# A two-layer decoder trunk in float32 on one core: a new order of work at three layer handovers and at the start

## Chip, core and metric

The kernel runs on one core of a Trainium2 chip (trn2). The metric is device time in microseconds of one execution of the whole program; lower is better. TensorE (PE) multiplies matrices, VectorE (DVE) and ScalarE (ACT) do the elementwise work, SyncE (SP) issues nearly all DMA transfers, GpSimd (POOL) a few.

## What is computed

A batch of one sequence, 256 tokens of width 2048, goes through two layers. Each layer is a mixer followed by a SwiGLU feed-forward of inner width 5632; every sublayer has an RMS norm in front (with shift and scale that depend on a vector `c`) and another one behind it (with a gate that depends on `c`).

```python
for layer in range(DEPTH):                       # DEPTH = 2
    sh1, sc1, g1, sh2, sc2, g2 = split(silu(c) @ mod_w[layer] + mod_b[layer])
    h = rms_norm(x, norm_g[layer, 0]) * (1 + sc1) + sh1
    y = nsa_mixer(h, ...) if layer == 0 else sb_mixer(h, k_sh, v_sh, ...)
    x = x + g1 * rms_norm(y, norm_g[layer, 1])
    h = rms_norm(x, norm_g[layer, 2]) * (1 + sc2) + sh2
    y = (silu(h @ W_gate) * (h @ W_up)) @ ffn_w_out[layer]
    x = x + g2 * rms_norm(y, norm_g[layer, 3])
```

Layer 0 mixes with block-sparse attention (compressed, selected and windowed keys), layer 1 with stick-breaking attention on keys and values that are projected once from the stream that leaves layer 0. All weights are float32 in HBM, 657 MB are moved in all.

## The kernel before

**Products.** Tokens are two tiles t = 0 and t = 1 of 128. A weight block is 512 rows by 512 columns (1 MB). It is loaded as `raw`; ACT copies it into `wh`, rounded to a shorter format, and DVE writes `wl` = raw - wh. Activations are split into a high and a low part in the same way. One unit is one weight block times one token tile: four 128-row pieces with three matmuls each (high·wh, high·wl, low·wh), 12 matmuls of 128x512 that add into one PSUM bank `acc`. The activation operands are called `hA`, `oA`, `hhF`, `hhK`, `hhB`, `oB`, `fa`; each has four chunks kt = 0 to 3 of 512 columns.

**Order of the work.** At build time a planner (class `Emit`, lines 149 to 422) lays down every instruction. It keeps a clock per engine from cost formulas, starts the next unit on PE when its plan has weights, operand and bank, and runs epilogues as coroutines (`run_bg`). `pump` (line 333) decides when the next weight block is split (`wq`), when a modulation row block is processed (`mq`), and when the next load is issued; pages of SBUF (21 of 8 KB per partition) are shared by loads, splits, activations and the rest. Where the plan has PE idle for over 1.2 us and a bank free, `fill` (line 194) puts in small matmuls on a scratch bank, named `idle`. On the chip only the order and the semaphores count.

**A handover** (`residual`, line 922) is the stretch between one sublayer's last product and the next one's first, and there are three: attention output to feed-forward in layer 0 (operand `hhF`), feed-forward of layer 0 to the key/value projection (`hhK`), attention output to feed-forward in layer 1 (`hhF`). For each token tile the chain is: sum of squares of the last block (`junk`), gate product (`z` or `yp`), reduce, square root, four updates of the residual stream `X` with their sums of squares, reduce, square root, reciprocal, four scaled chunks `xn`, 16 transposes on PE into `xT`, then per chunk four scale-and-shift operations `hf`, a rounding copy and a subtraction (`h_tile`, line 809; `split`, line 762). Tile 0 of a sublayer's last column block is multiplied four units ahead of tile 1 (`emit_lag`, line 1414), so tile 0's chain runs under tile 1's last 48 matmuls, and tile 1's chain under tile 0's first 48 of the next sublayer. While `E.urgent` is set, from the end of tile 0's product until tile 1's chunks are done, `pump` splits blocks in halves and stops when three units ahead have their weights:

```python
if self.wq and not (self.urgent and self.ahead > URGENT):      # URGENT = 2
```

When tile 0's first accumulator of the next sublayer ends, its epilogue is started at once (`after`, line 1671); for a feed-forward that is a silu on ACT (`sg`), for the key/value projection a copy (`pt`) and four transposes.

**Loads** are held back so that splits find pages:

```python
hold = 2 * max(0, self.reserve - len(self.ready)) + self.wait_pages
```

**Start** (lines 471 to 510). SP issues eight small loads, then `x` in two halves of 1 MB, three loads of constants, one of a bias, and then the modulation blocks `modq` (1 MB each) whose products with silu(c) give the first shift and scale; the first product of the kernel waits for four of them.

Of the kernel before, what the change touches and what calls it, by code (L numbers as in the profile page):

```python
# [18 lines left out]
P = 128  # L19
# [37 lines left out]
URGENT = 2  # L57
# [92 lines left out]
class Emit:  # L150
# [4 lines left out]
    def __init__(self, nc):  # L155
        self.now = 0.0
        self.clk = dict(PE=0.0, ACT=0.0, DVE=0.0, DMA=0.0, DMA2=0.0)
# [20 lines left out]
        self.urgent = False  # L178
# [5 lines left out]
        self.D = Engine(self, "DMA", nc.sync)  # L184
        self.D2 = Engine(self, "DMA2", nc.gpsimd)
# [147 lines left out]
    def pump(self):  # L333
# [4 lines left out]
        if self.wq and not (self.urgent and self.ahead > URGENT):  # L338
# [110 lines left out]
def kernel(ctx: ExitStack, tc, consts, x, c, mod_w, mod_b, norm_g, ffn_w_in, ffn_w_out, a_w_in,  # L449
# [43 lines left out]
    DMA.dma_start(L0[:, 0:512], consts[:, C_COS:C_END])  # L493
    DMA.dma_start(w2, a_cmp_w2[0].rearrange("s (m p) d -> p s m d", p=P))
    DMA.dma_start(gb[0:3 * H], a_gate_b.rearrange("o r -> r o"))
# [6 lines left out]
    for r in range(2):  # L502
        V.tensor_copy(maskb[:, r], cm[:, C_MASK - C_KEEP:C_MASK - C_KEEP + P])
    V.tensor_copy(maskTb, cm[:, C_MASKT - C_KEEP:C_MASKT - C_KEEP + P])
    for t in range(2):
        for r in range(4):
            V.tensor_copy(cmpb[:, t, r], cm[:, C_CMP - C_KEEP + 16 * t:C_CMP - C_KEEP + 16 * t + 16])
    E.put("s2")
    E.filler = (identb, maskb.rearrange("p r n -> p (r n)"))
# [287 lines left out]
    def xT_block(t, kt, r):  # L797

        xn = yield from E.get("s2", "xn")
        scaled(xn, X[:, t, kt * NB:(kt + 1) * NB], r)  # L800
# [8 lines left out]
    def h_tile(name, t, kt, r, a, sh):  # L809

        b = yield from xT_block(t, kt, r)
        dst = (yield from page_of((name, kt), "h" + name))[:, :, :, t * P:(t + 1) * P]
        hf = yield from E.get("s2", "hf")
        for j in range(4):
            cc = kt * 4 + j
            affine(hf[:, j * P:(j + 1) * P], b[:, j * P:(j + 1) * P], a[:, cc:cc + 1], sh[:, cc:cc + 1])
        E.put("x")
        split(dst, hf.rearrange("p (j n) -> p j n", j=4))
        E.put("s2")
        E.flag((name, kt, t))  # L820

    def h_all(name, t, r, a, sh, deps, pause=None):
        yield from E.wait(*deps)
        for kt in range(KT):
# [3 lines left out]
            else:  # L828
                E.spawn(h_tile(name, t, kt, r(), a, sh))
# [92 lines left out]
    def residual(key, t, nxt, final=False):  # L922
# [25 lines left out]
        if not final:  # L948
# [4 lines left out]
            if t == 1:  # L953
                yield from E.wait(*[(name, kt, 1) for kt in range(KT)])
                E.urgent = False
# [662 lines left out]
    E.spawn(start_norm())  # L1618
    E.spawn(make_xpe(0))
# [25 lines left out]
    def mm_unit(i, u):  # L1645
# [8 lines left out]
        def piece(j):  # L1654
# [9 lines left out]
            if j == js[-1]:  # L1664
                if u["stop"]:
                    E.spawn(after(u["epi"](accs.pop(u["acc"]), t, u["nb"]), E.fin + 0.1), front=True)
# [4 lines left out]
    def after(gen, t):  # L1671
        yield t
        yield from gen
# [73 lines left out]
```

## Time and profile before

| | |
|---|---|
| median of 3 runs | 2462.58 us (2462.18 to 2463.68) |
| profiled execution, its own time | 2461.23 us |
| its span, first to last instruction | 2459.4 us |
| PE busy | 97% of the span |
| DVE busy | 67% |
| ACT busy | 43% |
| DMA queue of SP | 73.4% of 16 engines, 651.59 MB |
| the chain that ended last | PE 84%, DVE 7%, ACT 4%, DMA 2% |

The time of an execution is its span and 1.8 us around it. A matmul's recorded duration overlaps that of the next one, so PE counts as busy through gaps that are shorter than a record; where PE really stood still is read from start times in the timeline. Small filler matmuls count as busy too.

### The profile page before, as it was taken

To read this page: it belongs to the slowest core of one execution; us is meant where nothing else is said; L and a number is where in the kernel's file an instruction comes from. 1 tells how busy PE (TensorE), PEld (TensorE's weight loads), DVE (VectorE), ACT (ScalarE), POOL (GpSimd) and SP (SyncE) were. 2 spreads that over 40 slices of the span, in tenths; PEclk is the share of its full clock that TensorE was granted. 3 is DMA by queue.
4 is the path that set the end of the run, shared out by engine and by line. 5 is a ranking of instruction groups with operands and counts; after the bars stand their busy time and mean duration, and the time that the engine had idled before them with its cause. 6 is when DMAs were issued, how large, how long until landed. Compare 5 with 4: busy or idle time off the path is not lost.

```text
span 2459.4 us, 27413 instructions
## 1 busy us (share of the span) xinstructions
PE 2387.1 (97%) x11238; PEld 1927.8 (78%) x11238; DVE 1638.2 (67%) x1373; ACT 1067.2 (43%) x1191; POOL 4.9 (0%) x12
## 2 busy tenths in 40 slices
PE   5999999999999999999999999999999999999998
PEld 3667776778888888888877888888788888888887
DVE  3788788968677667767768687666644544554554
ACT  3433444464333344333445365655433333433342
POOL 0000000000000000000000000000000000000000
PEclk9999999999999999999999999999999999999999
DMA  9996966868987689977667979675665646865642
GB/s 338 389 386 215 354 240 241 302 244 329 349 296 276 238 292 398 342 283 285 246 232 280 392 248 382 234 266 188 232 220 199 205 154 223 309 205 198 211 171 103
DMA packets 265629, 657.56 MB, mean 267 GB/s; under 512 B 12448, under 2 KB 30112, under 8 KB 240160
## 3 DMA queue, kind: packets, MB, share of 16 engines
q1 hardware_dynamic: 264800, 651.59, 73.4%
q0 software_dynamic: 704, 4.23, 0.5%
q8 instruction: 88, 1.44, 0.2%
q14 instruction: 37, 0.30, 0.0%
HBM read 653.64 MB, written 2.13 MB: 267 GB/s over the span
## 4 chain that ended last, share of the span: by engine, by line
PE 84%; DVE 7%; ACT 4%; DMA 2%; SPq 1%; issue 1%; DVEq 0%; ACTq 0%
PE acc L118 77%; DVE wl L118 2%; DVE macc L118 2%; PE z L118 1%; SPq L118 1%; ACT wh L118 1%; DMA modw<-in_mod_w_dram 1%; PE aT L118 1%; ACT hf L118 1%; PE oT L118 1%; PE sc L118 1%; ACT junk L118 1%; PE qacc L118 1%; PE pmod L118 1%; PE xT L118 1%
## 5 line engine op out<-in xcount | busy, mean ns | idle before, releaser
L118 DVE TENSOR_TENSOR wl<-raw,wh 128x2048 fp32r<-128x2048 f32 (+2 forms) x392 | 878.8, 2249 | 539.2 <-ACT wh L118 499.3
L118 ACT ACTIVATE wh<-raw 128x2048 fp32r<-128x2048 f32 (+2 forms) x392 | 732.8, 1880 | 653.1 <-PE acc L118 426.5
L118 PE MATMUL acc<-wh,hhF 128*128 128x512 f32 x2816 | 881.2, 391 | 0.0
L118 PEld LDWEIGHTS acc<-wh,hhF 128*128 128x128 f32 x2816 | 528.5, 188 | 113.7 <-issue 4.2
L118 PE MATMUL acc<-wl,hhF 128*128 128x512 f32 x1408 | 548.0, 389 | 0.0
L118 DVE SCALAR_TENSOR_TENSOR macc<-modw,cact,macc 128x2048 f32<-128x2048 f32 x180 | 422.4, 2347 | 44.5 <-DMA modw<-in_mod_w_dram 34.2
L118 PE MATMUL acc<-wh,fa 128*128 128x512 f32 x1408 | 437.1, 390 | 0.0
L118 PEld LDWEIGHTS acc<-wh,fa 128*128 128x128 f32 x1408 | 264.3, 188 | 55.5 <-issue 0.8
L118 PEld LDWEIGHTS acc<-wl,hhF 128*128 128x128 f32 x1408 | 264.5, 188 | 53.5
L118 PE MATMUL acc<-wl,fa 128*128 128x512 f32 x704 | 273.9, 389 | 0.0
L118 PE MATMUL acc<-wh,hA 128*128 128x512 f32 x640 | 222.6, 408 | 2.8 <-DVE hA L118 1.7
L118 PE MATMUL acc<-wh,hhK 128*128 128x512 f32 x512 | 164.1, 396 | 2.4 <-ACT hhK L118 1.8
L118 PEld LDWEIGHTS acc<-wh,hA 128*128 128x128 f32 x640 | 122.1, 191 | 44.6 <-issue 18.7
L118 PEld LDWEIGHTS acc<-wl,fa 128*128 128x128 f32 x704 | 132.2, 188 | 27.2
L118 PE MATMUL acc<-wl,hA 128*128 128x512 f32 x320 | 127.3, 398 | 2.0 <-DVE wl L118 2.0
L118 PEld LDWEIGHTS acc<-wh,hhK 128*128 128x128 f32 x512 | 96.8, 189 | 24.1 <-ACT hhK L118 2.0
L118 PE MATMUL acc<-wl,hhK 128*128 128x512 f32 x256 | 100.6, 393 | 2.3 <-DVE wl L118 2.3
L118 ACT ACTIVATE fa<-aT 128x512 fp32r<-128x512 f32 x44 | 26.0, 593 | 170.6 <-PE aT L118 158.6
L118 PE MATMUL acc<-wh,oA 128*128 128x512 f32 x256 | 84.9, 402 | 0.0
L118 PE MATMUL acc<-wh,hhB 128*128 128x512 f32 x256 | 84.8, 398 | 0.0
L118 PE MATMUL acc<-wh,oB 128*128 128x512 f32 x256 | 81.8, 394 | 0.0
L118 PEld LDWEIGHTS acc<-wl,hA 128*128 128x128 f32 x320 | 61.4, 192 | 13.5 <-DVE wl L118 3.6
(182 smaller groups left out, 1700.5 us busy)
## 6 DMA issues: line engine op xcount, KB each, us to landing
raw<-in_ffn_w_in_dram SPq DMA_DIRECT2D x176, 1024.0 KB, 5.4
modw<-in_mod_w_dram SPq DMA_DIRECT2D x160, 1024.0 KB, 7.2
raw<-in_ffn_w_out_dram SPq DMA_DIRECT2D x88, 1024.0 KB, 5.2
raw<-in_a_w_in_dram SPq DMA_DIRECT2D x40, 1024.0 KB, 13.0
modq<-in_mod_w_dram SPq DMA_DIRECT2D x32, 1024.0 KB, 14.1
modw<-in_kv_mod_w_dram SPq DMA_DIRECT2D x32, 1024.0 KB, 5.9
raw<-in_kv_w_dram SPq DMA_DIRECT2D x32, 1024.0 KB, 9.1
raw<-in_a_w_out_dram SPq DMA_DIRECT2D x16, 1024.0 KB, 7.4
```

The source lines that it names most:

```text
L118: return f(*a, **k)
```

## The change

Five edits, in one diff.

1. A sublayer's first operand chunk (kt = 0) is made first and in two steps of 256 columns, and its first half is enough to start PE. Its scaled copy `xn` is always DVE's.
2. `E.urgent` gets two levels. Level 1 (tile 0's chain) no longer stops weight splits; level 2 (tile 1's chain) does as before.
3. The epilogue of tile 0's first accumulator in the two feed-forwards and the key/value projection waits until the handover is over.
4. `hold` counts only as many missing splits as there are loads on their way or waiting for a split.
5. At the start `x` is issued from ACT's DMA queue, and the constants, `w2` and the bias behind the first seven blocks instead of ahead of them.

```diff
-URGENT = 2
+URGENT = (9, 9, 2)
...
-        if self.wq and not (self.urgent and self.ahead > URGENT):
+        if self.wq and self.ahead <= URGENT[self.urgent]:
...
-            hold = 2 * max(0, self.reserve - len(self.ready)) + self.wait_pages
+            hold = 2 * max(0, min(self.reserve - len(self.ready), len(self.wq) + 0)) + self.wait_pages
...
+    E.DA.dma_start(X[:, 0], xv[:, 0])
+    E.DA.dma_start(X[:, 1], xv[:, 1])
...
-    DMA.dma_start(X[:, 0], xv[:, 0])
-    DMA.dma_start(X[:, 1], xv[:, 1])
-    DMA.dma_start(cm[:, 0:C_COS - C_KEEP], consts[:, C_KEEP:C_COS])
...
+    def late_consts():
+
+        while E.dma_ptr < 6:
+            yield False
+        DMA.dma_start(cm[:, 0:C_COS - C_KEEP], consts[:, C_KEEP:C_COS])
+        DMA.dma_start(L0[:, 0:512], consts[:, C_COS:C_END])
+        DMA.dma_start(w2, a_cmp_w2[0].rearrange("s (m p) d -> p s m d", p=P))
+        DMA.dma_start(gb[0:3 * H], a_gate_b.rearrange("o r -> r o"))
+        yield E.when(cm)
...
-        scaled(xn, X[:, t, kt * NB:(kt + 1) * NB], r)
+        if first:
+            V.tensor_scalar(xn, X[:, t, kt * NB:(kt + 1) * NB], r, None, op0=OP.mult)
+        else:
+            scaled(xn, X[:, t, kt * NB:(kt + 1) * NB], r)
...
+        for i in range(0, 4, 2 if first else 4):
+            js = range(i, i + (2 if first else 4))
+            for j in js:
+                cc = kt * 4 + j
+                affine(hf[:, j * P:(j + 1) * P], b[:, j * P:(j + 1) * P], a[:, cc:cc + 1], sh[:, cc:cc + 1])
+            split(dst[:, :, js.start:js.stop], hf.rearrange("p (j n) -> p j n", j=4)[:, js.start:js.stop])
+            if i == 0:
+                E.flag((name, kt, t))
...
-            E.urgent = True
+            E.urgent = 1
...
+            E.urgent = 2
...
+                    first = u["acc"][0] in ("g0", "g1", "kv") and u["nb"] == 0 and t == 0
+                    E.spawn(after(u["epi"](accs.pop(u["acc"]), t, u["nb"]), E.fin + 0.1, first), front=True)
...
-    def after(gen, t):
+    def after(gen, t, calm=False):
         yield t
+        while calm and E.urgent:
+            yield False
```

**First place: the start.** SP's order before, from the constants that PE's first transposes need (`K`); the numbers behind a name tell buffers of one kind apart:

```order
L118 DMA K<-in_consts_dram 128x260
L118 DMA X<-in_x_dram 128x2048 x2
L118 DMA cmask_69<-in_consts_dram 128x288
L118 DMA L_3_82<-in_consts_dram 128x512
L118 DMA L_3_82<-in_a_cmp_w_dram 128x4x128
L118 DMA gb<-in_a_gate_b_dram 48x1
L118 DMA modq_134<-in_mod_w_dram 128x8x256
```

The same stretch of SP's order now:

```order
L118 DMA K<-in_consts_dram 128x260
L118 DMA modq_119<-in_mod_w_dram 128x8x256
L118 DMA modq_121<-in_mod_w_dram 128x8x256
L118 DMA modq_123<-in_mod_w_dram 128x8x256
L118 DMA raw_125<-in_a_w_in_dram 128x4x512
L118 DMA modq_127<-in_mod_w_dram 128x8x256
L118 DMA raw_129<-in_a_w_in_dram 128x4x512
L118 DMA modq_131<-in_mod_w_dram 128x8x256
L118 DMA cmask_69<-in_consts_dram 128x288
L118 DMA L_3_81<-in_consts_dram 128x512
L118 DMA L_3_81<-in_a_cmp_w_dram 128x4x128
L118 DMA gb<-in_a_gate_b_dram 48x1
```

And ACT's first instructions now, with the semaphore that each waits for (DMAHW0 is the one that the first half of `x` raises when it has landed):

```order
L118 DMA X<-in_x_dram 128x2048
L118 DMA X<-in_x_dram 128x2048 [waits DMAHW0_49]
L118 ACT_TABLE_LOAD
L118 ACTIVATE cact<-vecT 128x16 [waits DVE_49]
```

Both halves of `x` went to ACT's queue, the second behind the landing of the first, and three constant loads and the bias went behind seven blocks.

**Second place: the first handover on DVE.** Before, from tile 0's last operand chunk to the reduce that begins tile 1's chain (`z_3636` is tile 1's last gate product; `wl` of 128x1024 is half a split):

```order
L118 TENSOR_TENSOR hhF_682_4006<-hf_4007,hhF_682_4006 128x4x128
L118 TENSOR_TENSOR wl_4027<-raw_3873,wh_4026 128x1024
L118 TENSOR_TENSOR z_3636<-acc_3890,G_3105 128x512
L118 TENSOR_TENSOR wl_4027<-raw_3873,wh_4026 128x1024
L118 TENSOR_TENSOR wl_4049<-raw_3932,wh_4048 128x1024 x2
L118 TENSOR_REDUCE stat<-stat 128x1
```

Now, tile 0's first chunk (the first row is its last scaled copy):

```order
L118 TENSOR_SCALAR xn_3978<-X,stat 128x512
L118 TENSOR_TENSOR wl_3981<-raw_3896,wh_3980 128x1024
L118 TENSOR_TENSOR hhF_678_3987<-hf_3988,hhF_678_3987 128x2x128
L118 CAST hhF_678_3987<-hf_3988 128x2x128
L118 TENSOR_TENSOR hhF_678_3987<-hf_3988,hhF_678_3987 128x2x128
```

and from its last chunk to the reduce:

```order
L118 TENSOR_TENSOR hhF_685_4021<-hf_4022,hhF_685_4021 128x4x128
L118 TENSOR_TENSOR wl_3981<-raw_3896,wh_3980 128x1024
L118 TENSOR_TENSOR z_3617<-acc_3898,G_3150 128x512
L118 TENSOR_TENSOR wl_4062<-raw_3933,wh_4061 128x1024 x2
L118 TENSOR_REDUCE stat<-stat 128x1
```

One half split moved from between `z` and the reduce to the place ahead of tile 0's first chunk; two are left behind `z` where three were.

**Third place: the first handover on ACT, tile 1.** Before, from the scaled copy on (`sg` is the silu of the feed-forward's first accumulator):

```order
L118 ACTIVATE xn_4106<-X,stat 128x512
L118 ACT_TABLE_LOAD
L118 ACTIVATE sg_4120<-acc_4030 128x512
L118 ACTIVATE hf_4155<-xT_4133,mall 128x128 x3
L118 ACTIVATE hf_4162<-xT_4138,mall 128x128 x3
```

Now:

```order
L118 ACTIVATE xn_4116<-X,stat 128x512
L118 ACTIVATE hf_4146<-xT_4131,mall 128x128
L118 ACTIVATE hhF_678_3987<-hf_4146 128x2x128
L118 ACTIVATE hf_4146<-xT_4131,mall 128x128 x2
L118 ACTIVATE hf_4160<-xT_4136,mall 128x128 x3
```

The table load and the silu stand eleven operations later, behind the last chunk and a weight copy. On PE the fillers of the three handovers go from 16, 31 and 16 to none, 24 and none; in the rest of the program they go from 109 to 117.

## Rows read from the trace of the kernel before

**Rows 1.** Who PE waited for, whole span: total us, times, longest us.
```profile
PE qacc L118 <- DMA modq<-in_mod_w_dram: 13.5, 5, 10.0
PE acc L118 <- DVE wl L118: 10.1, 10, 4.1
```
**Rows 2.** Timeline, PE, first handover: start us, us, what [idle before <-releaser].
```profile
538.41 0.39 PE L118 MATMUL acc<-wh,hhF 128*128 128x512 f32 x1
...
549.30 0.72 PE L118 MATMUL idle<-maskb,identb 128*128 128x256 bf16 x5
552.57 3.41 PE L118 MATMUL xT<-K,xn 128*128 128x128 f32 x16 [2.55 <-DVE xn L118]
...
557.11 0.50 PE L118 MATMUL acc<-wh,hhF 128*128 128x512 f32 x1
```
**Rows 3.** Timeline, DVE, first handover.
```profile
533.74 0.73 DVE L118 TENSOR_SCALAR hf<-xT,mall 128x128 f32<-128x128 f32 x2 [0.74 <-ACT hf L118]
...
535.45 0.69 DVE L118 TENSOR_TENSOR hhF<-hf,hhF 128x512 fp32r<-128x512 f32 x1
...
540.97 0.69 DVE L118 TENSOR_TENSOR hhF<-hf,hhF 128x512 fp32r<-128x512 f32 x1 [0.70 <-ACT hhF L118]
...
543.67 3.49 DVE L118 TENSOR_TENSOR wl<-raw,wh 128x1024 fp32r<-128x1024 f32 x3
547.07 0.15 DVE L118 TENSOR_REDUCE stat<-stat 128x1 f32<-128x4 f32 x1
```
**Rows 4.** Timeline, ACT, first handover, tile 1.
```profile
552.76 1.28 ACT L118 ACT_TABLE_LOAD   x1
...
554.63 2.20 ACT L118 ACTIVATE hf<-xT,mall 128x128 f32<-128x128 f32 x6
```
**Rows 5.** Timeline, PE, second handover.
```profile
1297.02 0.50 PE L118 MATMUL acc<-wh,hhK 128*128 128x512 f32 x1 [0.65 <-ACT wh L118]
1298.28 0.50 PE L118 MATMUL acc<-wl,hhK 128*128 128x512 f32 x1 [0.76 <-DVE wl L118]
...
1303.64 2.90 PE L118 MATMUL idle<-maskb,identb 128*128 128x256 bf16 x25
1307.05 1.53 PE L118 MATMUL xT<-K,xn 128*128 128x128 f32 x12 [0.50 <-DVE xn L118]
...
1311.87 0.50 PE L118 MATMUL acc<-wh,hhK 128*128 128x512 f32 x1 [1.76 <-ACT hhK L118]
```
**Rows 6.** Timeline, DVE, second handover.
```profile
1297.00 4.63 DVE L118 TENSOR_TENSOR wl<-raw,wh 128x1024 fp32r<-128x1024 f32 x4 [0.26 <-ACT wh L118]
```
**Rows 7.** Timeline, PE, third handover.
```profile
1722.91 0.72 PE L118 MATMUL idle<-maskb,identb 128*128 128x256 bf16 x5
1726.17 3.55 PE L118 MATMUL xT<-K,xn 128*128 128x128 f32 x16 [2.54 <-DVE xn L118]
...
1730.76 0.48 PE L118 MATMUL acc<-wh,hhF 128*128 128x512 f32 x1
```
**Rows 8.** Timeline, the start: SP's issues, and PE's first modulation product.
```profile
4.73 0.90 SPq L118 DMA_DIRECT2D X<-in_x_dram  x2
...
8.20 6.28 SPq L118 DMA_DIRECT2D modq<-in_mod_w_dram  x3
...
17.68 1.93 PE L118 MATMUL qacc<-modq,cact 128*32 128x256 f32 x16 [10.04 <-DMA modq<-in_mod_w_dram]
```
**Rows 9.** Stretches: length, busy PE, PEld, DVE, ACT, POOL, PEclk, DMA, GB/s.
```profile
0.00:10.00 10.00, 1.09 (x4) 0.72 (x4) 0.39 (x2) 1.28 (x1) 0.20 (x4) 1.00 0.54 180
10.00:20.00 10.00, 1.93 (x16) 0.67 (x16) 2.18 (x16) 5.12 (x14) 0.00 (x0) 1.00 1.07 360
100.00:200.00 100.00, 98.29 (x461) 71.89 (x460) 83.04 (x98) 35.65 (x31) 0.00 (x0) 1.00 0.94 347
```
**Rows 10.** Stretches with the TensorE clock lowered, same columns.
```profile
439.00:446.00 7.00, 5.03 (x12) 3.76 (x13) 6.76 (x14) 1.42 (x5) 0.00 (x0) 0.54 0.12 45
552.00:556.00 4.00, 3.43 (x18) 3.41 (x19) 3.49 (x9) 3.95 (x7) 0.00 (x0) 0.57 0.00 0
```

More of the change, by code (lines that the diff above doesn't have):

```diff
@@ L156, in __init__ @@
         self.now = 0.0
-        self.clk = dict(PE=0.0, ACT=0.0, DVE=0.0, DMA=0.0, DMA2=0.0)
+        self.clk = dict(PE=0.0, ACT=0.0, DVE=0.0, DMA=1.5, DMA2=0.0)
         self.cells = {}
@@ L177, in __init__ @@
         self.wait_pages = 0
-        self.urgent = False
+        self.urgent = 0
         self.table = None
@@ L184, in __init__ @@
         self.D = Engine(self, "DMA", nc.sync)
+        self.DA = Engine(self, "DMA", nc.scalar)
         self.D2 = Engine(self, "DMA2", nc.gpsimd)
@@ L492 @@
     gb = small("gb", 1)
-    DMA.dma_start(L0[:, 0:512], consts[:, C_COS:C_END])
-    DMA.dma_start(w2, a_cmp_w2[0].rearrange("s (m p) d -> p s m d", p=P))
-    DMA.dma_start(gb[0:3 * H], a_gate_b.rearrange("o r -> r o"))
     identb = small("identb", P, BF16)
@@ L501 @@
     V.tensor_copy(identb, ident)
[L502 to L509, printed above, removed]
+    def late_consts():
[6 more added lines that the diff above has]
+        yield E.when(cm)
+        for r in range(2):
+            V.tensor_copy(maskb[:, r], cm[:, C_MASK - C_KEEP:C_MASK - C_KEEP + P])
+        V.tensor_copy(maskTb, cm[:, C_MASKT - C_KEEP:C_MASKT - C_KEEP + P])
+        for t in range(2):
+            for r in range(4):
+                V.tensor_copy(cmpb[:, t, r], cm[:, C_CMP - C_KEEP + 16 * t:C_CMP - C_KEEP + 16 * t + 16])
+        E.put("s2")
+        E.filler = (identb, maskb.rearrange("p r n -> p (r n)"))
     ones = K[:, C_ONE:C_ONE + 1]
@@ L795, in sumsq, with xT_block @@
         E.put("s2")
-    def xT_block(t, kt, r):
+    def xT_block(t, kt, r, first=False):
         xn = yield from E.get("s2", "xn")
-        scaled(xn, X[:, t, kt * NB:(kt + 1) * NB], r)
+        if first:
+            V.tensor_scalar(xn, X[:, t, kt * NB:(kt + 1) * NB], r, None, op0=OP.mult)
+        else:
+            scaled(xn, X[:, t, kt * NB:(kt + 1) * NB], r)
         yield
@@ L807, in xT_block, with h_tile @@
         return b
-    def h_tile(name, t, kt, r, a, sh):
-        b = yield from xT_block(t, kt, r)
+    def h_tile(name, t, kt, r, a, sh, first=False):
+        b = yield from xT_block(t, kt, r, first)
         dst = (yield from page_of((name, kt), "h" + name))[:, :, :, t * P:(t + 1) * P]
         hf = yield from E.get("s2", "hf")
-        for j in range(4):
-            cc = kt * 4 + j
-            affine(hf[:, j * P:(j + 1) * P], b[:, j * P:(j + 1) * P], a[:, cc:cc + 1], sh[:, cc:cc + 1])
+        for i in range(0, 4, 2 if first else 4):
[6 more added lines that the diff above has]
+                E.flag((name, kt, t))
         E.put("x")
-        split(dst, hf.rearrange("p (j n) -> p j n", j=4))
         E.put("s2")
-        E.flag((name, kt, t))
     def h_all(name, t, r, a, sh, deps, pause=None):
@@ L828, in h_all @@
             else:
-                E.spawn(h_tile(name, t, kt, r(), a, sh))
+                E.spawn(h_tile(name, t, kt, r(), a, sh, kt == 0 and True))
     def start_norm():
@@ L954, in residual @@
                 yield from E.wait(*[(name, kt, 1) for kt in range(KT)])
-                E.urgent = False
+                E.urgent = 0
     kv = {}
@@ L1618 @@
     E.spawn(start_norm())
+    E.spawn(late_consts())
     E.spawn(make_xpe(0))
@@ L1665, in piece @@
                 if u["stop"]:
-                    E.spawn(after(u["epi"](accs.pop(u["acc"]), t, u["nb"]), E.fin + 0.1), front=True)
+                    first = u["acc"][0] in ("g0", "g1", "kv") and u["nb"] == 0 and t == 0
+                    E.spawn(after(u["epi"](accs.pop(u["acc"]), t, u["nb"]), E.fin + 0.1, first), front=True)
                 release(u, i)
         return Unit(u["key"], start_time, [lambda j=j: piece(j) for j in js])
-    def after(gen, t):
+    def after(gen, t, calm=False):
         yield t
+        while calm and E.urgent:
+            yield False
         yield from gen
```

## The prediction

> **What bounds the kernel now.** Read the page first: PE counts as busy 97% of the span, DVE 67%, ACT 43%. Then the stretches: from 100 to 200 us PE is busy 98.29 of 100 while the DMA engines run at a 0.94 share [rows 9]. The product work itself is not touched by the change, so what can be won are the places where PE stands still. The list of waits names the two large ones by releaser, modulation loads and late weight splits [rows 1], but it misses time, since fillers and the recorded length of a matmul hide gaps. So the timeline of PE is read last, by start times, at the three handovers and at the start.
>
> At the first handover PE's last product of tile 0 is followed by fillers at 549.30, transposes at 552.57, and the next product at 557.11: 7.8 us in which only 16 transposes are useful [rows 2]. The second has the same picture, 1303.64 to 1311.87 or 8.2 us, and before it PE waited twice more for splits, the last time until 1298.28 [rows 5]. The third: 1722.91 to 1730.76, 7.8 us [rows 7]. At the start PE's first modulation product waits 10.04 us, until 17.68 [rows 8].
>
> **Handovers, the chain up to the transposes.** Tile 1's chain begins with a reduce on DVE. Before, three half splits stand between the gate product and that reduce: they begin at 543.67 and last 3.49, 1.16 each, and the reduce starts at 547.07 [rows 3]. In the new order one of the three stands ahead of tile 0's first chunk, so two remain: -1.16. What the moved half costs there: DVE waits 0.74 for ACT just at that place, and four more times down to the last wait of 0.70 [rows 3] in the alternation of the two engines on tile 0's chunks. I walked the new order with the durations of these rows and of their neighbours: the half fills the first gap, the two-step chunk adds one rounding copy and one subtraction of half size, and the last chunk's subtraction ends about 1.1 earlier, because ACT no longer waits for the half behind it. That puts the reduce about 2.4 earlier. Bounds: 1.16 if DVE's gaps only move, 2.4 by the walk. I take 2.3. Tile 0 itself has room: its first chunk ends at 535.45 + 0.69 = 536.1 and PE takes it at 538.41 [rows 2, 3], 2.3 us for a half split of 1.16.
>
> **Handovers, from transposes to product.** Before: 552.57 to 557.11 = 4.54 [rows 2]. In between ACT loads a table (1.28) and runs a silu, and reaches the first `hf` only at 554.63 [rows 4], and chunk 0 is needed whole. Now the silu and its table load come after the chunks. What is left: 16 transposes, which at the pace of the second handover (12 in 1.53, [rows 5]) take about 2.0, and under them one `hf` on each engine, a half rounding and a half subtraction, each at most the 0.69 of a whole one [rows 3]. I take 2.2, so -2.3. Bounds: if the clock is low during the transposes they alone take 3.41 [rows 2] and the gain is 1.1; no gain is better than down to 2.0.
>
> First handover: -2.3 - 2.3 = **-4.6**; between -2.3 and -5.9 (7.8 less 2.0 of transposes). The third has the same rows, with 1726.17 to 1730.76 = 4.59 [rows 7]: **-4.7**, between -2.3 and -5.9. At the second, four half splits of 4.63 in all stand between the gate product and the reduce [rows 6]; the new order has three, and another half now stands ahead of tile 1's first addition, so weights are there when PE asks and the waits of 0.65 and 0.76 [rows 5] go. By the same walk the reduce moves by 2.5. From transposes to product it was 4.82 (1307.05 to 1311.87, with a copy for the keys and four extra transposes in between [rows 5]), now 2.2: **-5.1**, between -2.3 and -8.
>
> What is late next: by these numbers the transposes start 0.7 to 0.9 us behind PE's last product, so the chain still ends last, by little. The delayed silu holds one PSUM bank and nobody waits for it: the accumulators that follow have other banks, and splits for the next block are needed only 48 matmuls later.
>
> **The start.** SP issues `x` at 4.73 and the first modulation block at 8.20 [rows 8], and in the first 10 us the DMA engines move 180 GB/s, in the next 10 they are full at 360 [rows 9]. Now ACT's first two instructions are the issues of `x`, and SP reaches the first block where `x` stood, at 4.73. The blocks start up to 3.5 us earlier (8.20 - 4.73). Against that stands that the second half of `x` is issued only when the first has landed, and that it shares the engines with the blocks. The constants move behind seven blocks; their readers come later (a few small casts on DVE, which no longer stand ahead of `vecT`). ACT is blocked until the first half of `x` lands, but had nothing to do in the first 10 us but one instruction of 1.28 [rows 9]. I take **-3.0**, between 0 and -3.5. While loads limit, PE keeps what it gets earlier, and from 100 on it has next to no gap in which to lose it [rows 9].
>
> The Trainium skill speaks against this part: "DMA: Bandwidth & Descriptors", section "Rules for kernel authors", says that spreading DMAs over several issuing engines brings no bandwidth, since all run on the same 16 engines, and saves only the sequencer's issue time. By it the term would be at most the issue time ahead of `x`, the 3.5 us that are my upper bound, and less for whatever the blocks lose to `x`.
>
> **Page rule and fillers elsewhere.** The rule for loads and the new start rearrange the planner's order everywhere. What can be counted: 8 more fillers outside the handovers, at 0.11 each (25 in 2.90, [rows 5]): **+0.9**. The layer-0 attention, 340 to 460 us, is where this can go either way; one late split there held PE 4.1 us [rows 1] and the clock stood at 0.54 over 439 to 446, which costs another 3.2 [rows 10]. One such wait more or less is +7 or -7; I take none.
>
> **Sum.** 2461.23 (the profiled execution) - 4.6 - 5.1 - 4.7 - 3.0 + 0.9 = 2444.7. The median of the runs lies 1.35 above the profiled execution, so **2446 us**.
>
> **Rivals.**
>
> *The clock falls where fillers are gone* (chance 0.15). The handovers lose 39 fillers. In the first one the clock was at 0.57 from 552 to 556 [rows 10] after PE had waited 2.55 us [rows 2], and the transposes ran at 1.2 GHz. Speaking against: the idle time that I expect is under 1 us. If it falls at all three, half of the 3.41 that the transposes took there [rows 2], 1.7 each: 2446 + 5 = 2451. The Trainium skill has this as a rule: "TensorE: Matmul & The Clock Gate", section "Why this matters for your kernels", warns that idle gaps between bursts of matmuls bring the array back to half clock.
>
> *DVE is in series* (0.13). The split work is moved, not removed; if tile 0's chunks slow down by what was moved, the reduce is where it was, and only the second half of each handover is won: 2446 + 2.3 + 2.5 + 2.3 = 2453.
>
> *The start wins nothing* (0.13): `x` and the first blocks share the engines, and the fourth block lands when it did: 2449.
>
> *Slower: late splits in the attention of layer 0* (0.05). Pages that were held for splits now go to loads, and a split without two free pages waits. The price is 7.3 us each (4.1 of wait, 3.2 of clock). The order has fillers in five places there, where it had three. It decides from the third extra wait on: 22 us, 2446 + 22 = 2468.
>
> *The other way* (0.04): the wait of rows 1 and others in that stretch vanish: 2438.
>
> **How the numbers follow.** The forecast with its own range, 2441 to 2450, has 0.5. The clock, series and start cases lie between 2449 and 2453, or at 2457 where two meet. So 2437 to 2457 holds 8 in 10. A measurement tells about 0.2% or 4.9 us from no change, so faster means under 2457.7: 0.89. Within 0.2%: 0.06; slower: 0.05.
>
> **What would show it.** Right: at each handover the next product starts within 3.5 us of the last one, tile 1's reduce comes with two half splits (three at the second) behind the gate product, and no table load stands between `xn` and `hf`; PE's first modulation product starts near 13 and its first weight product 3 us earlier. Wrong: clock rows under 1.0 during the handovers, a reduce that did not move, or a layer-0 attention from 340 to 460 that got longer by more than the start gave.

## The result and the profile after

The changed kernel takes **2437.18 us** (median of 4 runs, 2435.52 to 2439.67) against 2462.38 beside it on the same chip. The ratio is 0.9895, 95% interval 0.9882 to 0.9908: 25 us faster, where 16.6 were forecast. The direction is right, but the median lies 3.8 us under the forecast's own range (2441 to 2450) and only 0.2 inside the wide one (2437 to 2457), and the sum came out for partly wrong reasons: the handovers gave less than forecast, and a part priced at nothing gave more than all of them.

The profiled execution took 2436.0 us (span 2434.2). The first table follows PE through both traces by the start of the same products; a difference that grows between two lines was won between them.

| PE's product | before | after | difference |
|---|---|---|---|
| first modulation product | 17.68 | 14.28 | -3.4 |
| first weight product, layer 0 | 33.13 | 29.88 | -3.25 |
| first attention output product | 412.32 | 408.80 | -3.5 |
| first of the feed-forward, layer 0 | 538.41 | 524.98 | -13.4 |
| tile 1's first there | 557.11 | 541.45 | -15.7 |
| last with `hhF`, layer 0 | 1172.62 | 1158.72 | -13.9 |
| first with `hhK` | 1290.13 | 1272.72 | -17.4 |
| tile 1's first there | 1311.87 | 1290.46 | -21.4 |
| first of the feed-forward, layer 1 | 1712.02 | 1688.89 | -23.1 |
| tile 1's first there | 1730.76 | 1705.37 | -25.4 |
| end of the span | 2459.45 | 2434.22 | -25.2 |

So the start gave 3.3 to 3.5, the three handovers 2.2, 4.0 and 2.3, or 8.5 together, and 10 came in a stretch of which the prediction said that it took nothing for it: between the first attention output product and the feed-forward.

Who PE waited for, after (us in total, times, longest). The 4.1 us wait for a weight split [rows 1] is gone, and a new one for `sg` stands there:

```profile
PE acc L118 <- DVE wl L118: 5.7, 9, 1.5
...
PE aT L118 <- DVE sg L118: 2.2, 1, 2.2
```

The stretch from 412 to 538 us (length, busy PE, PEld, DVE, ACT, POOL, PEclk, DMA share, GB/s), first before, then after:

```profile
412.00:538.00 126.00, 119.57 (x582) 93.47 (x581) 105.33 (x128) 62.36 (x108) 1.57 (x2) 0.96 0.77 279
```

```profile
412.00:538.00 126.00, 122.36 (x599) 96.55 (x597) 110.11 (x138) 69.63 (x128) 0.55 (x1) 1.00 0.80 288
```

PE is busy 2.8 us more, and its clock is never lowered, where it stood at 0.54 from 439 to 446 before [rows 10] and at 0.50 from 426 to 429. (After the change the last 13 us of this window are already the feed-forward.)

The first handover after the change, timeline of PE, ACT and DVE from tile 0's last product on (start, length, what, and what the engine waited for):

```profile
535.63 0.39 PE L118 MATMUL acc<-wh,hhF 128*128 128x512 f32 x1
...
538.13 3.57 PE L118 MATMUL xT<-K,xn 128*128 128x128 f32 x16 [2.12 <-DVE xn L118]
539.34 0.46 ACT L118 ACTIVATE hf<-xT,mall 128x128 f32<-128x128 f32 x1 [1.03 <-PE xT L118]
539.84 0.41 DVE L118 TENSOR_SCALAR hf<-xT,mall 128x128 f32<-128x128 f32 x1 [0.97 <-ACT hf L118]
540.28 0.42 ACT L118 ACTIVATE hhF<-hf 128x256 fp32r<-128x256 f32 x1 [0.48 <-DVE hf L118]
...
541.45 0.47 PE L118 MATMUL acc<-wh,hhF 128*128 128x512 f32 x1
```

Against [rows 2] the fillers are gone, the transposes start 2.5 us behind the last product's start (before 3.5) and still run at half clock, 3.57 us, so the next product comes 3.3 behind their first and not 2.2. The clock in that stretch:

```profile
538.00:542.00 4.00, 3.87 (x19) 3.79 (x20) 2.24 (x7) 2.49 (x7) 0.00 (x0) 0.57 0.00 0
```

DVE in front of tile 1's reduce. First two rows of before, which lie between those of [rows 3], then the rows after:

```profile
541.92 1.23 DVE L118 TENSOR_TENSOR wl<-raw,wh 128x1024 fp32r<-128x1024 f32 x1 [0.26 <-ACT wh L118]
543.07 0.68 DVE L118 TENSOR_TENSOR z<-acc,G 128x512 f32<-128x512 f32 x1
```

```profile
528.63 1.22 DVE L118 TENSOR_TENSOR wl<-raw,wh 128x1024 fp32r<-128x1024 f32 x1
529.76 0.68 DVE L118 TENSOR_TENSOR z<-acc,G 128x512 f32<-128x512 f32 x1
530.37 2.35 DVE L118 TENSOR_TENSOR wl<-raw,wh 128x1024 fp32r<-128x1024 f32 x2
532.63 0.15 DVE L118 TENSOR_REDUCE stat<-stat 128x1 f32<-128x4 f32 x1
```

Two half splits instead of three stand behind `z`, as the order said. But `z` starts 4.78 us behind tile 0's first product (524.98), and before it was 4.66 (543.07 against 538.41): the half that moved ahead of the chunks brought `z` no sooner. The reduce comes 7.65 behind that product instead of 8.66, 1.0 sooner.

The second handover, after, to be read against [rows 5]:

```profile
1284.70 2.79 PE L118 MATMUL idle<-maskb,identb 128*128 128x256 bf16 x24
1288.30 1.97 PE L118 MATMUL xT<-K,xn 128*128 128x128 f32 x16 [0.81 <-DVE xn L118]
1290.46 0.50 PE L118 MATMUL acc<-wh,hhK 128*128 128x512 f32 x1 [0.19 <-ACT hhK L118]
```

Here fillers were left and the clock stayed: 16 transposes in 1.97 us and the product 2.2 behind the first of them, as forecast.

### The profile page after: what moved, and what is told of

Its sections match the earlier page's. It is cut to its first block, busy times and chain, and to the rows that moved or that the text cites. A ratio compares the mean times of both kernels' runs of the same rounds, so it can differ in the third digit from the quotient of the medians.

```text
span 2434.2 us, 27343 instructions
## 1 busy us (share of the span) xinstructions
PE 2377.7 (98%) x11207; PEld 1922.8 (79%) x11207; DVE 1633.8 (67%) x1364; ACT 1075.4 (44%) x1212; POOL 4.5 (0%) x12
## 3 DMA queue, kind: packets, MB, share of 16 engines
HBM read 653.64 MB, written 2.13 MB: 269 GB/s over the span
## 4 chain that ended last, share of the span: by engine, by line
PE 86%; DVE 6%; ACT 4%; DMA 2%; SPq 1%; issue 1%; DVEq 0%; ACTq 0%
PE acc L118 79%; DVE wl L118 2%; PE z L118 1%; ACT wh L118 1%; DVE macc L118 1%; DMA modw<-in_mod_w_dram 1%; SPq L118 1%; PE aT L118 1%; PE sc L118 1%; PE oT L118 1%; PE qacc L118 1%; ACT hf L118 1%; PE xT L118 1%; ACT junk L118 1%; PE pmod L118 1%
## 5 line engine op out<-in xcount | busy, mean ns | idle before, releaser
L118 PEld LDWEIGHTS acc<-wl,hA 128*128 128x128 f32 x320 | 61.2, 191 | 13.9 <-DVE wl L118 4.3
```

The lines of the kernel that those rows point to most:

```text
L118: return f(*a, **k)
```

## The experiments

### Which edit gave what

Two theories of the unexpected 10 us: P, the page rule (loads go out sooner), or S, the moved start (which re-deals everything the planner does later). The edits were run one group at a time.

The page rule alone:

```diff
-            hold = 2 * max(0, self.reserve - len(self.ready)) + self.wait_pages
+            hold = 2 * max(0, min(self.reserve - len(self.ready), len(self.wq) + 0)) + self.wait_pages
```

> The kernel before with the new page rule for loads and nothing else. After the whole change the first product of layer 0's feed-forward started 13.4 us earlier (538.41 to 524.98), of which 3.5 were there when the attention output products began. Theory P: the page rule makes the other 9.9, since loads go out sooner and no split is late in the layer-0 attention. Then this kernel reaches that product near 528.5 and takes about 2462.4 - 10 - 3 (the wait at 1239 us goes too) = 2450 us. Rival S: the moved start re-deals the planner's order there, and the page rule alone does little: the product stays within 2 us of 538.4 and the time is between 2459 and 2464.

Measured: 2447.38 us against 2462.69, ratio 0.9934 (0.9916 to 0.9951). The attention output products begin 2.75 us later than before and the feed-forward 7.0 earlier, at 531.43, so the stretch between them shrank by 9.7. The 2.75 are within the noise: five kernels of this document whose instruction order is the same up to the first handover (the one before and the runs of the handover edits below, together and each alone) begin these products anywhere from 408.57 to 413.25. The stretch itself is steady, 125.8 to 126.6 us in all seven traces with the old rule and 116.2 to 117.4 in all eight with the new one. From the last `hhF` product to the first with `hhK`, 1173 to 1290 before, the page rule won another 3.0; before, PE stood there for 2.9 us on `mrow` of a modulation. The changed kernel with the old rule put back:

> The changed kernel with the old page rule put back. Theory P: it loses what the page rule gave, the first product of the feed-forward comes near 535 and the time is about 2437 + 10 + 3 = 2450 us. Rival S: it keeps that gain, the product comes near 525 and the time is between 2435 and 2441 us.

Measured: 2452.63 us, 15.5 above the changed kernel. From the first attention output product to the feed-forward it takes 125.8 us, where the kernel before takes 126.1 and the changed one 116.2. By the medians the page rule is worth 15.3 us alone and 15.5 on top of the rest (its profiled execution, the longest of its four, has a span 11.5 us shorter than the one before); the rival falls.

How it does that is seen in DVE's order and in SP's issues. DVE before, from the split of the attention output product's first weight block to that of its second (more `macc` rows lie between those shown):

```profile
409.74 2.29 DVE L118 TENSOR_TENSOR wl<-raw,wh 128x2048 fp32r<-128x2048 f32 x1 [0.15 <-ACT wh L118]
415.93 2.35 DVE L118 SCALAR_TENSOR_TENSOR macc<-modw,cact,macc 128x2048 f32<-128x2048 f32 x1
...
436.37 2.34 DVE L118 SCALAR_TENSOR_TENSOR macc<-modw,cact,macc 128x2048 f32<-128x2048 f32 x1
438.64 2.28 DVE L118 TENSOR_TENSOR wl<-raw,wh 128x2048 fp32r<-128x2048 f32 x1
```

and with the page rule alone, where the first row holds the last split of the product before and the first block's, and the second row the second block's:

```profile
405.72 4.59 DVE L118 TENSOR_TENSOR wl<-raw,wh 128x2048 fp32r<-128x2048 f32 x2 [1.10 <-ACT wh L118]
...
416.96 2.29 DVE L118 TENSOR_TENSOR wl<-raw,wh 128x2048 fp32r<-128x2048 f32 x1 [2.40 <-ACT wh L118]
```

Before, no split began for 29 us, and the second block's, for which PE waited from 436.9 on, stood behind a row of modulation products. SP's issue of that block and, in a fence of its own, ACT's copy of it before; then the issue with the page rule:

```profile
412.49 0.38 SPq L118 DMA_DIRECT2D raw<-in_a_w_out_dram  x1
```

```profile
431.43 1.91 ACT L118 ACTIVATE wh<-raw 128x2048 fp32r<-128x2048 f32 x1
```

```profile
405.01 0.38 SPq L118 DMA_DIRECT2D raw<-in_a_w_out_dram  x1
```

The issue comes 7.5 us earlier, and the block lands 5.8 earlier (5.4 us behind its issue before, 7.0 with the rule). That alone doesn't make the split late: before, the block had been in SBUF for 13.5 us when ACT began to copy it. The larger part is its place in the order. `pump` takes up a split only once it has issued the block's load; pages were kept free for splits of blocks that were not even on their way, so the load was put off, and meanwhile the plan had laid the modulation products into DVE's order, ahead of the split. With the new rule the `wl` comes 22 us earlier, and with it the wait and the lowered clock behind it go.

One block more of caution in the changed kernel's rule:

```diff
-min(self.reserve - len(self.ready), len(self.wq) + 0)
+min(self.reserve - len(self.ready), len(self.wq) + 1)
```

> The changed kernel with the page rule one block more cautious (pages also held for one block that is not on its way). Theory P: weight loads for the attention's output product go out later again, the wait in the layer-0 attention comes back in part: the feed-forward's first product between 527 and 535 instead of 525 and a time between 2440 and 2450 us. Rival: one block more is harmless, the deadlines are met either way, 525 and 2437 us.

Measured: 2443.00 us, 5.8 above the changed kernel; the feed-forward's first product at 530.77, and the stretch in front of it takes 121.3 us, half way between the two rules. The dose acts in the expected sense.

The new start alone:

> The kernel before with the new start alone (x from ACT's queue, constants behind seven blocks). Both theories: the first modulation product about 3.4 us earlier, at 14.3. Theory P: that is all, the first product of the feed-forward comes at 535.0 and the time is about 2459 us. Rival S: the attention gains 9.9 as well, the product comes near 525 and the time is about 2449 us.

Measured: 2456.87 us against 2462.69, ratio 0.9977 (0.9967 to 0.9987). The first modulation product stands at 14.33 and the feed-forward's first product at 532.95, 2.0 better than the 535.0 of theory P and far from 525. What is better lies before the first attention output product, where executions of one and the same order differ by more than that; behind it the stretch takes 126.6 us, and the wait of 4.0 us for a late split is there as before.

The second queue was tried apart from the later constants, in the changed kernel with `x` back on SP behind `K`:

```diff
-    E.DA.dma_start(X[:, 0], xv[:, 0])
-    E.DA.dma_start(X[:, 1], xv[:, 1])
...
     DMA.dma_start(K, consts[:, 0:C_KEEP])
+    DMA.dma_start(X[:, 0], xv[:, 0])
+    DMA.dma_start(X[:, 1], xv[:, 1])
```

> The changed kernel with both halves of x issued by SP again, behind the last small load, the constants still behind seven blocks. Theory Q: with its own queue x moves while the engines were nearly idle in the first 5 us; without it x's 2 MB stand ahead of the blocks in the stream, and PE's first modulation product comes 2 to 3 us later than 14.3, the time is about 2439.5 us. Rival I (the second queue saves only issue time): 0.9 later, for SP's two issues, at 15.2, and 2438 us.

Measured: 2438.53 us (2436.91 to 2439.02); the first modulation product at 15.81, 1.5 later than after the whole change and so between the two theories; in the time of a run the 1.4 us are not clear of the noise. The first stretches of the trace after the whole change, then with `x` on SP:

```profile
0.00:5.00 5.00, 0.00 (x0) 0.00 (x0) 0.17 (x1) 0.00 (x0) 0.20 (x4) 1.00 0.59 214
5.00:10.00 5.00, 1.11 (x4) 0.71 (x4) 1.06 (x4) 1.70 (x3) 0.00 (x0) 1.00 0.77 236
```

```profile
0.00:5.00 5.00, 0.00 (x0) 0.00 (x0) 0.17 (x1) 1.28 (x1) 0.20 (x4) 1.00 0.16 43
5.00:10.00 5.00, 1.09 (x4) 0.72 (x4) 1.06 (x4) 0.21 (x1) 0.00 (x0) 1.00 0.92 315
```

SP's issue of the first blocks, in the same order:

```profile
6.42 4.75 SPq L118 DMA_DIRECT2D modq<-in_mod_w_dram  x3
```

```profile
5.67 6.86 SPq L118 DMA_DIRECT2D modq<-in_mod_w_dram  x3
```

The second queue fills the first 5 us, 214 GB/s instead of 43, but in the next five the engines are less full, 236 instead of 315. Of the 3.4 us at the first modulation product 1.9 came from the constants' place (17.68 to 15.81) and 1.5 from the queue. The rule quoted from the Trainium skill, "DMA: Bandwidth & Descriptors", section "Rules for kernel authors", that more issuing engines bring no bandwidth, agrees from 10 us on: the rate from 10 to 15 us is 366 GB/s with two queues and 377 with one. What was won is issue time, which the rule leaves: with one queue SP comes to `x` only at 4.73, behind its small loads, while ACT issues it at 0.7. The block's own issue is not what counts, for with two queues it is later (6.42 instead of 5.67) and the product still comes sooner.

### The handovers

The three edits of the handovers alone:

> The kernel before with the three handover edits (chunk 0 in two steps, two levels of urgency, delayed epilogue), old page rule and old start. Nothing can differ before 520 us. Theory now, from the trace after the change (gaps between tile 0's last and tile 1's first product 8.0 to 5.8, 8.5 to 6.0 and 8.1 to 5.8, and 1.5 in tile 0's first units at the second): 2.2 + 4.0 + 2.3 = 8.5 saved, about 2454 us. Rival, the prediction's own terms: 4.6 + 5.1 + 4.7 = 14.4, about 2448 us, the rest being given back by the page rule and the start.

Measured: 2453.97 us against 2462.69, ratio 0.9969 (0.9958 to 0.998): 8.7 us, as now expected. (The three groups alone add up to 15.3 + 5.8 + 8.7 = 29.8 us, against 25.2 together; the difference is within their intervals.) The profiled execution was the longest of its ten (2460.92), yet its handovers show more than that: from tile 0's first to tile 1's first product 15.4, 17.8 and 15.4 us, where it was 18.7, 21.7 and 18.7 before and 16.5, 17.7 and 16.5 after the whole change. The 1.1 us between the two is the clock: in this execution it was lowered only from 553.76 on, and 16 transposes take

```profile
552.56 2.57 PE L118 MATMUL xT<-K,xn 128*128 128x128 f32 x16 [2.11 <-DVE xn L118]
554.77 0.78 PE L118 MATMUL acc<-wh,hhF 128*128 128x512 f32 x1
```

The execution lost 5 us again in the feed-forward behind it, where PE waits 2.2 us for `sg` and the clock is at 0.50 once more from 636 to 639.

Then each edit alone. A gap is here the time from the start of tile 0's last product to that of tile 1's first: 8.05, 8.46 and 8.08 us at the three handovers before, 5.82, 5.99 and 5.83 after the whole change. The net gain is counted from tile 0's first product to tile 1's first. Chunk 0 first and in two steps:

> The kernel before with only chunk 0 first and in two steps. Before, the three gaps from tile 0's last to tile 1's first product are 8.04, 8.46 and 8.08 us; after the whole change 5.82, 5.99 and 5.83. Theory now (the parts overlap): the silu and its table load still hold ACT for 1.9 us, so chunk 0's first half comes at most 0.9 earlier, and the reduce does not move: gaps near 7.2. Rival, the prediction's walk: half of its 2.3 in the second part comes from here and DVE is freed earlier for the reduce: gaps near 6.2.

Measured: 2458.66 us, ratio 0.9988 (0.9979 to 0.9997). Gaps of 4.75, 5.79 and 4.75, below both expectations, but the gap alone deceived: tile 0's first 48 products now take 12.65 instead of 10.65, because PE waits for splits that the old urgency rule still stops:

```profile
545.15 0.50 PE L118 MATMUL acc<-wh,hhF 128*128 128x512 f32 x1 [0.67 <-ACT wh L118]
546.41 0.50 PE L118 MATMUL acc<-wl,hhF 128*128 128x512 f32 x1 [0.76 <-DVE wl L118]
```

Net 1.3, 3.1 and 1.35 us. From the first transpose (550.39) to the product (552.20) it takes 1.81 us here, at full clock and with the silu and its table load on ACT meanwhile. The two levels of urgency alone:

> The kernel before with only the two levels of urgency. Theory now: one half split goes ahead of tile 0's chunks and the reduce of tile 1 moves by one half split, 1.0 to 1.2: gaps near 7.0, if the split that stood behind the gate product is really the one that moved. Rival, the walk of the prediction: 2.3 to 2.4, gaps near 5.7. Second rival: nothing moves without the two-step chunk, since tile 0's chain is as long as before: gaps at 8.0.

Measured: 2457.02 us, ratio 0.9976 (0.9965 to 0.9987); gaps of 6.34, 8.66 and 6.34, which no theory named. Tile 0's products do not wait more than before, the reduce comes 7.4 us behind tile 0's first product (8.66 before), and the transposes run at full clock: net 1.7, 1.1 and 1.75 us, 1.3 of the first by the reduce and the rest by the clock. So the half split is worth about its length, and the two edits belong together: the one makes the chunk early, the other lets the splits through that it would starve.

The delayed epilogue alone:

> The kernel before with only the delayed epilogue of tile 0's first accumulator. Theory now: transposes at half clock (3.41 us) and the whole of chunk 0 still stand between tile 1's scaled copies and the product, so 4.5 becomes about 4.0: gaps 7.5 at the first and third handover. Rival, the prediction's view: ACT gets the 1.9 us of table load and silu back in full: gaps near 6.2.

Measured: 2462.18 us against 2462.12, ratio 0.9995 (0.9984 to 1.0005): nothing. The gaps grew, to 8.79, 8.46 and 8.79. Both expectations were wrong, and the timeline says why. ACT is free now, so the planner deals the scale-and-shift operations of a chunk to ACT and DVE in turn:

```profile
555.01 0.46 ACT L118 ACTIVATE hf<-xT,mall 128x128 f32<-128x128 f32 x1 [1.03 <-PE xT L118]
555.51 0.41 DVE L118 TENSOR_SCALAR hf<-xT,mall 128x128 f32<-128x128 f32 x1 [0.97 <-ACT hf L118]
555.96 1.51 ACT L118 ACTIVATE hf<-xT,mall 128x128 f32<-128x128 f32 x4 [0.48 <-DVE hf L118]
556.45 0.41 DVE L118 TENSOR_SCALAR hf<-xT,mall 128x128 f32<-128x128 f32 x1 [0.53 <-ACT hf L118]
```

Each start is 0.45 to 0.50 behind the other engine's. Before, with ACT held by the table load, DVE did four in a row from 553.72 to 554.69, 0.32 apart.

So the changed kernel was run with that one edit undone, the epilogue started at once:

```diff
-                    E.spawn(after(u["epi"](accs.pop(u["acc"]), t, u["nb"]), E.fin + 0.1, first), front=True)
+                    E.spawn(after(u["epi"](accs.pop(u["acc"]), t, u["nb"]), E.fin + 0.1, False), front=True)
```

> The changed kernel with the epilogue of tile 0's first accumulator started at once again. Theory now, from the run with the two-step chunk alone: DVE makes the first half of chunk 0 by itself while ACT loads the table, so the delay wins nothing; the gaps at the first and third handover stay at 5.8 with the clock at half during the transposes, or 4.7 where it isn't, and the time is within 2 us of 2437. Rival, the prediction: ACT's 1.9 us of table load and silu come back between transposes and product, gaps of 7 to 7.7 and about 2442 us.

Measured: 2433.42 us (2430.93 to 2436.82), gaps of 4.29, 6.03 and 4.31: better than expected. As the changed kernel's own runs were on another chip, both were run once more side by side:

> The changed kernel itself, unaltered, beside the next one on the same chip. Both theories: 2437 us, gaps at the first and third handover of 5.8 with the granted clock at half in the transposes or 4.7 where it isn't, a wait of 2.4 for the silu product near 618 us.

> The changed kernel with the epilogue of tile 0's first accumulator started at once, unaltered from the run before. Theory D (the delay is a loss): gaps of 4.3 at the first and third handover, no wait near 618 us, 3 to 4 us less than the changed kernel on the same chip, about 2433.5. Rival: the 3.8 us between the medians were the difference of two chips, and the two kernels agree within 1 us here.

Measured: 2437.13 us (2436.65 to 2439.95) for the changed kernel and 2433.39 us (2433.08 to 2435.41) without the delay. The delayed epilogue costs 3.7 us. The first handover without it:

```profile
539.54 1.97 PE L118 MATMUL xT<-K,xn 128*128 128x128 f32 x16 [2.10 <-DVE xn L118]
539.73 1.28 ACT L118 ACT_TABLE_LOAD   x1
540.23 0.73 DVE L118 TENSOR_SCALAR hf<-xT,mall 128x128 f32<-128x128 f32 x2
540.99 0.29 DVE L118 CAST hhF<-hf 128x256 fp32r<-128x256 f32 x1
541.03 0.60 ACT L118 ACTIVATE sg<-acc 128x512 f32<-128x512 f32 x1
...
541.34 0.50 PE L118 MATMUL acc<-wh,hhF 128*128 128x512 f32 x1
```

ACT loads its table and runs the silu, and nobody waits for it: DVE makes the half chunk alone, 1.05 us from its first `hf` to the end of the rounding copy. After the change the same piece goes ACT, DVE, ACT and takes 1.36 (539.34 to 540.70). Most of the rest lies in the feed-forward. With the delay, DVE has a modulation product in front of the product with `sg`:

```profile
620.40 2.34 DVE L118 SCALAR_TENSOR_TENSOR macc<-modw,cact,macc 128x2048 f32<-128x2048 f32 x1
622.66 0.68 DVE L118 TENSOR_TENSOR sg<-sg,acc 128x512 f32<-128x512 f32 x1
```

and without it behind:

```profile
618.30 0.68 DVE L118 TENSOR_TENSOR sg<-sg,acc 128x512 f32<-128x512 f32 x1
618.90 2.34 DVE L118 SCALAR_TENSOR_TENSOR macc<-modw,cact,macc 128x2048 f32<-128x2048 f32 x1
```

In the first case PE waits 2.2 us for `sg`; in the second that wait is not there. The clock adds to it. In this execution with the delay it stood at 0.50 from 624 to 627, right behind the wait, and layer 0's feed-forward took 619.7 us from tile 1's first product to the last with `hhF`, against 616.0 without the delay; in the first profiled execution of the change, where it did not fall there, 617.3. Between 500 and 2400 us the clock never falls in the three executions without the delay. In six of the seven with the delay and the other handover edits it does, at a handover, behind this wait or at both. No run tells whether the delay makes it fall.

The clock. The changed kernel with 20 fillers put back ahead of tile 1's transposes, all other orders as they were:

```diff
+        if first == 2 and t == 1:
+            o = yield from E.get("x", "idle")
+            at = E.clk["PE"], E.fin
+            for _ in range(20):
+                T.matmul(o[:, 0:2 * P], *E.filler, start=True, stop=True)
+            E.clk["PE"], E.fin = at
+            E.put("x")
...
-        b = yield from xT_block(t, kt, r, first)
+        b = yield from xT_block(t, kt, r, first and (2 if name[:2] == "hF" else 1))
```

> The changed kernel with 20 filler matmuls put back ahead of tile 1's transposes at the first and third handover; every other engine's order is the same. There PE stood idle for 2.3 us, the granted clock fell to half for 3.41 us and the 16 transposes took 3.3. Theory C: with fillers the clock stays, the transposes take 2.0, the first hf starts some 0.4 earlier, and the next product comes 0.5 to 0.6 us sooner, then set by the operand (gap from tile 0's last to tile 1's first product 5.8 down to 5.2), about 2436 us in all. Rival: the operand's chain on ACT and DVE sets the product already, the transposes end earlier and the gap stays at 5.8, 2437 us. In the time of a run both are within the noise; the gap in the trace tells them apart.

Measured: 2437.14 us, gaps of 4.73 and 4.66 where they were 5.82 and 5.83:

```profile
537.84 2.36 PE L118 MATMUL idle<-maskb,identb 128*128 128x256 bf16 x20
540.21 1.94 PE L118 MATMUL xT<-K,xn 128*128 128x128 f32 x16
542.34 0.50 PE L118 MATMUL acc<-wh,hhF 128*128 128x512 f32 x1 [0.19 <-ACT hhF L118]
```

The transposes take 1.94 instead of 3.57 and the gap shrinks by 1.1, twice what was expected; the operand is what sets the product now, 2.1 behind the first transpose. In the time of a run nothing is left of it, and the second execution of the changed kernel shows why: there the gaps were 4.98 and 4.65 without any filler. The clock does not fall at these places each time, so fillers insure against something that happens in some executions only.

The two together, no delay and 20 fillers:

> The changed kernel without the delayed epilogue and with 20 filler matmuls ahead of tile 1's transposes at the first and third handover. Theory now: full clock in the transposes, gaps of 4.3 to 4.7 there (1.1 or more under 5.8 each), about 2435 us. Rival, the prediction's view of ACT: gaps of 6 to 6.6, about 2439 us.

Measured: 2434.37 us (2431.44 to 2436.09), gaps of 4.35 and 4.30: no more than without the fillers. The best version of all is the change without the delayed epilogue, 2433.4 us.

## Why the prediction was right and wrong

**The page rule: priced at nothing, and the largest term.** The step that failed is "One such wait more or less is +7 or -7; I take none". The wait was in hand, 4.1 us [rows 1], and so was the clock at 0.54 behind it [rows 10]. What was not asked is why that split was late: the rule that the change loosens had held its load back, and with it its place in DVE's order. The prediction made of this a rival with the opposite sign (loads would take pages from splits), and gave the right sign 0.04. Measured 15.3 us alone; in the traces 9.7 to 9.9 of it lie between the first attention output product and the feed-forward and 3 near 1239 us. The price of a wait was short as well: the clock stood at 0.50 a second time in that stretch, from 426 to 429, an estimated 1.7 us more than the 4.1 + 3.2 of the prediction, so 9.0 of the 9.9.

**Handovers: -14.4 forecast, -8.5 in the profile after.** (Its bound of -5.9 for the first is 7.8 less 2.0, so -5.8.) Three steps:

- "That puts the reduce about 2.4 earlier" was the upper bound; the lower one, 1.16 for a half split, was right (1.0 measured). The walk let the moved half fill a gap of DVE and tile 0's last chunk end 1.1 sooner. It did not: the chunk's last subtraction ended 3.25 us behind tile 0's first product before (540.97 + 0.69 [rows 3]) and ends 3.73 behind it after, with DVE still waiting for ACT over the chunks. A half split follows it, and `z` stands right behind that on DVE, as before. What was won is the half split that no longer stands behind `z`.
- From transposes to product -2.3 was forecast. With the clock up it is -2.4 (2.13 with fillers against 4.54), with the clock down -1.2. The rival on the clock, at 0.15, was there at two of three handovers of the profiled execution, with 1.1 us each instead of its 1.7, since with the clock up the operand sets the product. Its argument, idle time under 1 us, failed with the reduce: PE waited 2.12 us for `xn`. The trace agrees with the section named there, "TensorE: Matmul & The Clock Gate" of the Trainium skill, "Why this matters for your kernels", in part: the fall followed both idle gaps in one execution and one of the two in another of the same program.
- The reason given, that the silu and its table load come out of the way, was wrong in itself. It was read from an ACT row that stood between two others in time [rows 4], but no row shows the product waiting for ACT there. What stood between on PE were eleven fillers, behind the transposes of [rows 2]; on DVE the operand's high part, which the product takes first, was being rounded meanwhile:

```profile
555.81 1.36 PE L118 MATMUL idle<-maskb,identb 128*128 128x256 bf16 x11
```

```profile
555.12 0.43 DVE L118 CAST hhF<-hf 128x512 fp32r<-128x512 f32 x1
```

That part was ready at 555.55, so the fillers held the product up, by an estimated 1.3 us (557.11 - 555.81), about the 1.2 won here with the clock down. The planner puts fillers where its plan has PE waiting, here for the whole of chunk 0; with the half chunk it puts none. So the gain belongs to the half chunk, and in the run with that edit alone the product follows 1.81 behind the first transpose though the silu and its table load are where they were. That nobody waits for the delayed silu was wrong too: its delay cost 3.7 us.

The second handover was forecast at -5.1 and gave -4.0. Its second half was right (from transposes to product 4.82 became 2.16), and again the reduce moved less: 1.3 instead of 2.5, counted from tile 0's first product. Of the waits for splits in tile 0's units, 1.5 of 2.6 went (13.28 to 11.75 us for 48 products that need 10.65).

**The start: the size right, the path only in part.** -3.0 forecast, -3.4 measured at the first product, -3.25 at the first weight product, and the upper bound of 3.5 held. But the term was worked out from SP reaching the first block at 4.73, and SP reaches it at 6.42, 1.8 earlier than before and not 3.5. What counted, by the run with `x` on SP, is the data ahead of the block. The three constant loads are 672 KB by their shapes, which at the 360 GB/s of [rows 9] makes an estimated 1.9 us, and 1.9 is what the constants' place gave; the other 1.5 came from `x`, which moves while the engines had little else to do. So the good number is partly luck. The sign "near 13" does not follow from the prediction's own sum, which gives 17.68 - 3.0 = 14.7.

**Fillers elsewhere, +0.9:** not to be seen beside the rest. Their number says where the planner sees PE idle, not what PE loses.

**The sum.** Terms by the trace: start -3.3, handovers -8.5, attention -9.9, from tile 1's first product of layer 0's feed-forward to `hhK` -1.7 (with the new wait for `sg` in it), the rest -1.8: -25.2. That the time missed the forecast by no more than some 9 us is luck: two errors of opposite sign, -14.6 elsewhere and +5.9 at the handovers, met in part.

## What to carry to other kernels

Where an engine waits for prepared data, compare when the load was issued and landed with when the preparation began, and look at the rule that holds loads back: room reserved for work whose input has not been asked for delays that work itself, and in a planned order it also costs that work its place. An instruction that lies between two others in time is worth its length only if the consumer waits for its engine: taking it away can even cost, when a scheduler then deals a short chain to two engines that hand over at every step. And when two edits only work together, measure from a landmark ahead of both: here a gap shrank by 3.3 us while the products in front of it grew by 2.0.

## What had not been expected of the hardware

The same instruction order gives spans that differ by 4 us from one execution to another (2434.2 and 2438.2 for the changed kernel), and lowered clocks are part of it: behind the same wait of 2.1 us for `xn` at the first handover the granted clock was at half through the transposes in one execution (0.57 from 538 to 542) and fell only at 542.01, 0.9 us into them, in the other; at the third handover it fell in the first and stayed at 1.00 in the second. At these places a single profile can't price a stretch to better than about a microsecond, and over the first 410 us not to better than some 5 (408.57 to 413.25 for one and the same order). And a hand-over between ACT and DVE on neighbouring columns of one PSUM tile made the next operation start 0.45 to 0.50 us behind the one before, where operations in a row on DVE start 0.32 apart.
